# Queries and keys of twelve heads turned by DMA transposes of their 16-bit halves

## The chip, the cores and the metric

The kernel runs on one core of a Trainium2 chip. The core has five engines that work at the same time, each through its own queue in order: TensorE (PE; matrix products, results into PSUM), VectorE (DVE), ScalarE (ACT), GpSimd (POOL) and SyncE (SP, which here only issues DMAs). The metric is the device time in microseconds (us) of one execution; several runs are made and their median is given.

## The reference

One layer of a hybrid encoder over 256 tokens of width 2048, in float32:

```python
h = rms_norm(x)
p = h @ w_in                      # columns: qa, ka, va, fa (8 forget gates), qb, kb, vb
qa, ka = rms_norm per head        # 8 "fox" heads of width 128
out_a = softmax(qa.ka/sqrt(128) + c[t] - c[s], s <= t) @ va
out_b = stick_breaking(qb.kb/sqrt(128), s < t) @ vb          # 8 heads
x = x + concat(rms_norm(out_a), rms_norm(out_b)) @ w_out
x = x + ConvFFN(rms_norm(x))      # up 2048 -> 2 x 5632, causal conv, SiLU gate, down
```

The products q.k contract over the 128 features of a head, so q and k are needed with features on partitions and tokens along the free dimension. The projection leaves them the other way: a row tile holds 128 tokens on partitions and 4 heads x 128 features along the free dimension.

## The kernel before

**Products.** TensorE multiplies float32r data. To keep float32 accuracy each weight block of 128 x 2048 is loaded (w_raw, five buffers, issued by SyncE in `load`, L269), cast by ScalarE into a high part (w_hi, three buffers, `cast`, L275), and VectorE takes the rest (w_lo = w_raw - w_hi, `subtracted`, L283). `in_three` (L303) then makes three products per block: high with the activations' high and low parts (8 matmuls x 512 columns), and low with high (4 matmuls). So each block costs TensorE 12 matmuls, ScalarE one cast and VectorE one subtraction.

**Pieces.** The whole program is a list of steps (`steps`), each a weight block with its matmuls; here they are called pieces. The loop at the end emits, for piece n: evictions that are due (`following`), the cast and subtraction of piece n+2, the load of piece n+6, the matmuls of piece n, and then a tick. It thus writes out the order of each engine's queue by hand; nothing reorders it afterwards.

**Units.** After the fox values, five units of eleven pieces (0 to 10) project 512 + 512 columns each: unit 1 gives rows rA (q and k of fox heads 0 to 3), unit 2 rB (fox heads 4 to 7), unit 3 rC (q and k of stick-breaking heads 0 to 3), unit 4 the values vB, unit 5 rD (q and k of stick-breaking heads 4 to 7). A unit computes seven products for eight quarter blocks; the pieces 3, 5, 8 and 10 are double (24 matmuls, with a tick in the middle), the others single (12). Banks are called bank_a, bank_b, bank_c and bank_e. Pieces 0, 1, 2 and 3 of a unit open on bank_a, bank_c, bank_b and bank_e.

**Heads.** Beside the pieces run generators that are advanced once per tick. `fox_rows` and `sb_rows` take a finished unit's rows: the fox rows are normalised (squares on ScalarE, L662; a factor per head; the multiplication on VectorE, L672), and then `to_heads` transposes q and k: for k and then q, eight 128 x 128 transposes on TensorE into two PSUM tiles ps_h (L649), and a tick later two ScalarE evictions (L653), which also scale, into a tile kA, qA, kB or qB of 128 x 4 heads x 256 tokens (two buffers). After that one head every three ticks starts: scores ps_s (L744 to L750), exponentials (L762, L763), transposition ps_p (L774), eviction pT and p (L779, L780), product with the values ps_o (L721, L723), eviction oFox and its squares (L789, L727, L730). The stick-breaking heads have ps_z in place of ps_s. A gate sets when a half may be transposed: `started["fox"]` counts the fox heads whose scores have been emitted; rB waits for four, rC for eight.

In unit 5's first pieces the values are finished: `values_done` casts vB to its high part on ScalarE (L709) once VectorE has added the last bank (L605).

Of the kernel before, what the change touches and what calls it, by code (L numbers as in the profile page):

```python
# [8 lines left out]

F32 = mybir.dt.float32  # L10
F32R = mybir.dt.float32r
AF = mybir.ActivationFunctionType
ALU = mybir.AluOpType
AX = mybir.AxisListType

P = 128
D = 2048
S = 256
NT = S // P
KT = D // P  # L20
HD = 128
NH = 8
# [6 lines left out]
QSCALE = HD ** -0.5  # L29
# [17 lines left out]
def hybrid_layer(  # L47
# [19 lines left out]
    nc = tc.nc  # L67
    act, dve = nc.scalar, nc.vector
# [21 lines left out]
    class Early:  # L90
        n = 0
# [20 lines left out]
    gq = const.tile([P, 1], F32, name="gq")  # L112
    ccol = const.tile([P, 4, NC2], F32, name="ccol")
    R2 = const.tile([P, S], F32, name="R2")
    rstd1 = const.tile([P, NT], F32, name="rstd1")
    headR = const.tile([P, NH], F32R, name="headR")
    nrstd1 = const.tile([P, NT], F32, name="nrstd1")
    hT = big.tile([P, KT, 2, S], F32R, name="hT")
    xp = xf.rearrange("(t p) d -> p t d", p=P)
# [20 lines left out]
    g_q, g_k = pcol[:, 48:49], pcol[:, 49:50]  # L140
# [24 lines left out]
    def rsqrt(out_, ss, scale, n, gap=2):  # L165
        a = small.tile([P, n], F32, name="rs_a", tag=f"rs_a{n}")
        y = small.tile([P, n], F32, name="rs_y", tag=f"rs_y{n}")
        u = small.tile([P, n], F32, name="rs_u", tag=f"rs_u{n}")
        dve.tensor_scalar(a, ss, scale, EPS, op0=ALU.mult, op1=ALU.add)
        for _ in range(gap):  # L170
            yield
        act.activation(y, a, AF.Ln)
        act.activation(y, y, AF.Exp, scale=-0.5)
        dve.tensor_tensor(u, a, y, op=ALU.mult)
        dve.tensor_tensor(u, u, y, op=ALU.mult)
        dve.tensor_scalar(u, u, -0.5, 1.5, op0=ALU.mult, op1=ALU.add)
        dve.tensor_tensor(out_, y, u, op=ALU.mult)
# [20 lines left out]
    def split_tokens(ps, k, g, n=2):  # L198
        for j in range(n):
            i = k + j  # L200
            act.activation(hT[:, i, 0, :], ps[:, j, :], AF.Identity, scale=g[:, i : i + 1])
        for j in range(n):
# [6 lines left out]
    def squares(ss, c, junk):  # L209
        for t in range(NT):  # L210
            act.activation(
                junk, x2[:, t, c * 512 : (c + 1) * 512], AF.Square, accum_out=ss[:, t, c : c + 1]
            )
# [58 lines left out]
    def cast(raw, n, copy):  # L272
        hi = whi.tile([P, 2048], F32R, name="w_hi", tag="w_hi")
        lo = wlo.tile([P, 2048], F32R, name="w_lo", tag="w_lo")
        copy(hi[:, :n], raw[:, :n])  # L275
        return hi, lo
# [60 lines left out]
    oFox = late.tile([P, NH, S], F32, name="oFox")  # L337
    oSb = []
    ssq = [late.tile([P, S], F32, name=f"ssq{i}") for i in range(2)]
    masksR = at.tile([P, 4 * P], F32R, name="masksR")  # L340
    ntri = masksR[:, 2 * P :]
    maskF, maskB = (f32(masksR[:, i * P : (i + 1) * P]).unsqueeze(1).to_broadcast([P, 2, P]) for i in range(2))
    lf = at.tile([P, 4, NT, NH], F32, name="lf")[:, 0]
    chi = at.tile([P, S], F32R, name="chi")
    cR = at.tile([P, 3 * P], F32R, name="cR")
# [3 lines left out]
    def heads_tile(name):  # L349
        return at.tile([P, 4, S], F32, name=name, tag="qk", bufs=2)  # L350
# [8 lines left out]
    def evict_values(ps, c0, n):  # L359
        hi, lo, v1 = (v[:, c0 : c0 + n] for v in tile_of["vA"])  # L360
        act.activation(hi, ps[0][:, :n], AF.Identity, scale=rstd1[:, 0:1])
        act.activation(v1, ps[1][:, :n], AF.Identity, scale=rstd1[:, 1:2])

# [10 lines left out]
    started = {"fox": 0, "sb": 0}  # L374

    tile_of = {}
# [258 lines left out]
    def row_tiles(name, which):  # L635
# [2 lines left out]

        return make

    def to_heads(rows, keys, scales):

        for n in (1, 0):
            dst = tile_of[keys[n]] = heads_tile(keys[n])
            pss = []
            for t in range(NT):
                ps = psb.tile([P, 4, P], F32, name="ps_h", tag="t")
                for h in range(4):
                    nc.tensor.transpose(ps[:, h, :], rows[n, t][:, h * HD : (h + 1) * HD], ident)  # L649
                pss.append(ps)  # L650
            yield
            for t in range(NT):
                act.activation(dst[:, :, t * P : (t + 1) * P], pss[t], AF.Identity, scale=scales[n])  # L653

    def fox_rows(half):
        def done(rows):
            order = [(1, 0), (1, 1), (0, 1), (0, 0)]
            ss = small.tile([P, 4, 4], F32, name="ss", tag="ss")
            rn = small.tile([P, 4, 4], F32, name="rn", tag="rn")
            for m, nt in enumerate(order):  # L660
                for h in range(4):
                    act.activation(  # L662
                        zeros, rows[nt][:, h * HD : (h + 1) * HD], AF.Square,
                        accum_out=ss[:, m, h : h + 1],
                    )
                if m < 3:
                    yield
            flat = "p a b -> p (a b)"
            yield from rsqrt(rn.rearrange(flat), ss.rearrange(flat), 1.0 / HD, 16)
            for m, nt in enumerate(order):  # L670
                r3 = rows[nt].rearrange("p (h d) -> p h d", h=4)
                dve.tensor_tensor(r3, r3, rn[:, m, :].unsqueeze(2).to_broadcast([P, 4, HD]), op=ALU.mult)  # L672
                if m % 2:
                    yield
            while started["fox"] < 4 * half:
                yield
            yield from to_heads(rows, (f"qA{half}", f"kA{half}"), (gq, g_k))
            for h in range(4 * half, 4 * half + 4):
                waiting.append(fox_head(h, half))

        return done

    def sb_rows(half):
        def done(rows):
            while started["fox"] < NH or started["sb"] < 4 * half:
                yield
            if half:
                yield
                yield
            yield from to_heads(rows, (f"qB{half}", f"kB{half}"), (QSCALE, 1.0))  # L690
            ready.add(f"qB{half}")
            if "vB" in ready:
                start_sb(half)

        return done

    def start_sb(half):
        for h in range(4 * half, 4 * half + 4):
            waiting.append(sb_head(h, half))
# [737 lines left out]
```

## Time and profile before

| | |
|---|---|
| median of 3 runs (lowest, highest) | 1094.15 us (1093.35, 1094.19) |
| the profiled execution: its time, its span | 1093.69 us, 1091.6 us |
| busy: PE, PE weight loads, DVE, ACT, POOL | 1087.1, 939.8, 924.1, 755.3, 59.0 us |
| granted TensorE clock | 1.00 |
| moved by DMA | 258.53 MB, mean 237 GB/s |

"L275" is line 275 of the kernel before; a row such as `w_hi<-w_raw` names what is written and what is read, `x8` a number of instructions. Rows of the timeline begin with the start in us and the duration in us; adjacent equal instructions are merged, and `[1.33 <-PE ps_o L723]` says that the engine was idle for 1.33 us before and what ended that. The ends of matmuls are modelled, so the time from one start to the next is the better measure.

### The profile page before, as it was taken

The numbers are of one execution on the slowest core, as the hardware profiler recorded it, in microseconds if no ns is written. First come the engines' busy times: TensorE is split into PE (matmuls) and PEld (weight loads), VectorE is DVE, ScalarE is ACT, GpSimd is POOL, SyncE is SP. The second block draws the span as 40 slices with busy tenths as digits, with TensorE's granted clock in tenths as the row PEclk, the third lists the DMA queues.
The fourth block names the chain that finished last, engine by engine and source line by source line (L and its number), as shares of the span: only waits on it lengthen the run. The fifth ranks groups of instructions, "written<-read, shape, count | busy, mean of one in ns | idle before, by whom it ended". The sixth has DMA issues, their size and how long they took to land.

```text
span 1091.6 us, 14672 instructions
## 1 busy us (share of the span) xinstructions
PE 1087.1 (100%) x5701; PEld 939.8 (86%) x5701; DVE 924.1 (85%) x918; ACT 755.3 (69%) x968; POOL 59.0 (5%) x53
## 2 busy tenths in 40 slices
PE   9999999999999999999999999999999999999998
PEld 9988888888888888888888888888888888888887
DVE  5988899888897667779887988889898889879996
ACT  6767697767766657767766776677667667667763
POOL 0000000001000000000000000100000000000000
PEclk9999999999999999999999999999999999999999
DMA  8897886868777464669989597996979699895995
GB/s 310 275 271 240 271 205 205 246 192 265 236 215 250 154 199 160 212 173 248 289 204 316 176 264 253 255 296 170 301 197 282 229 246 281 212 319 163 295 251 149
DMA packets 175216, 258.53 MB, mean 237 GB/s; under 512 B 4633, under 2 KB 98219, under 8 KB 175147
## 3 DMA queue, kind: packets, MB, share of 16 engines
q1 hardware_dynamic: 151690, 210.26, 56.7%
q0 software_dynamic: 23280, 47.19, 24.5%
q8 instruction: 45, 0.74, 0.3%
q14 instruction: 25, 0.20, 0.0%
q10 hardware_dynamic: 176, 0.14, 0.0%
HBM read 255.48 MB, written 2.10 MB: 236 GB/s over the span
## 4 chain that ended last, share of the span: by engine, by line
PE 100%; DVE 0%; issue 0%
PE pu L1171 45%; PE bank_a L303 18%; PE bank_b L303 11%; PE bank_c L303 6%; PE acc_o L303 6%; PE acc_v L423 4%; PE bank_e L303 2%; PE acc L303 2%; PE ps_x L193 1%; PE ps_h L649 1%; PE ps_o L721 1%; PE ps_z L802 0%; PE ps_o L723 0%; PE ps_i L187 0%; PE half L303 0%; PE ps_z L821 0%
## 5 line engine op out<-in xcount | busy, mean ns | idle before, releaser
L283 DVE TENSOR_TENSOR w_lo<-w_raw,w_hi 128x2048 fp32r<-128x2048 f32 (+2 forms) x251 | 556.1, 2219 | 123.7 <-ACT w_hi L275 122.5
L275 ACT CAST w_hi<-w_raw 128x2048 fp32r<-128x2048 f32 (+2 forms) x251 | 464.6, 1854 | 222.2 <-PE pu L1171 91.7
L1171 PE MATMUL pu<-hT,w_hi 128*128 128x512 f32 x1408 | 333.6, 390 | 0.0
L1171 PEld LDWEIGHTS pu<-hT,w_hi 128*128 128x128 f32 x1408 | 263.1, 188 | 53.5
L1171 PEld LDWEIGHTS pu<-hT,w_lo 128*128 128x128 f32 x1408 | 180.0, 191 | 6.5
L1171 PE MATMUL pu<-hT,w_lo 128*128 128x256 f32 x1408 | 182.1, 283 | 0.0
L1224 POOL DMA_DIRECT2D w_raw<-in_w_down_dram x31 | 39.8, 1302 | 715.4 <-DVE w_lo L283 384.9
L1096 ACT ACTIVATE tap<-up,ccol 128x256 f32<-128x256 f32 x176 | 74.6, 495 | 0.0
L303 PE MATMUL bank_a<-w_hi,hT 128*128 128x512 f32 x192 | 48.6, 395 | 0.0
L303 PEld LDWEIGHTS bank_a<-w_hi,hT 128*128 128x128 f32 x192 | 35.2, 188 | 6.8
L303 PE MATMUL bank_a<-w_hi,s 128*128 128x512 f32 x160 | 40.0, 392 | 0.0
L303 PE MATMUL bank_b<-w_hi,s 128*128 128x512 f32 x160 | 40.0, 392 | 0.0
L303 PE MATMUL bank_a<-w_hi,g 128*128 128x512 f32 x152 | 38.0, 392 | 0.0
L423 PE MATMUL acc_v<-w_hi,hT 128*128 128x344 f32 x192 | 35.9, 329 | 0.0
L303 PEld LDWEIGHTS bank_b<-w_hi,s 128*128 128x128 f32 x160 | 28.9, 189 | 5.2
L303 PEld LDWEIGHTS bank_a<-w_hi,s 128*128 128x128 f32 x160 | 28.9, 189 | 5.2
L1101 DVE TENSOR_TENSOR val<-val,tap 128x512 f32<-128x512 f32 x44 | 30.3, 689 | 2.7 <-DVE val L1101 0.5
L1101 DVE TENSOR_TENSOR gate<-gate,tap 128x512 f32<-128x512 f32 x44 | 30.3, 689 | 2.6 <-DVE gate L1101 0.5
L303 PE MATMUL acc_o<-w_hi,oSb 128*128 128x512 f32 x128 | 31.8, 397 | 0.0
L1082 DVE TENSOR_TENSOR up<-t,R 128x512 f32<-128x512 f32 x44 | 30.5, 692 | 1.5
L303 PEld LDWEIGHTS bank_a<-w_hi,g 128*128 128x128 f32 x152 | 27.4, 189 | 4.9
L1089 ACT ACTIVATE gate<-up,ccol 128x256 f32<-128x256 f32 x44 | 24.1, 594 | 10.2 <-DVE s L1143 5.2
(293 smaller groups left out, 1413.9 us busy)
## 6 DMA issues: line engine op xcount, KB each, us to landing
w_raw<-in_w_up_dram SPq DMA_DIRECT2D x88, 1024.0 KB, 7.4
w_raw<-in_w_down_dram SPq DMA_DIRECT2D x44, 1024.0 KB, 6.6
w_raw<-in_w_in_dram SPq DMA_DIRECT2D x40, 1024.0 KB, 5.3
w_raw<-in_w_down_dram POOLq DMA_DIRECT2D x31, 1024.0 KB, 9.9
w_raw<-in_w_out_dram SPq DMA_DIRECT2D x16, 1024.0 KB, 7.6
w_raw<-in_w_in_dram POOLq DMA_DIRECT2D x10, 1024.0 KB, 9.8
w_raw<-in_w_in_dram SPq DMA_DIRECT2D x13, 516.0 KB, 5.0
xb<-in_x_dram POOLq DMA_DIRECT2D x4, 512.0 KB, 8.7
```

Of the source, the lines that this page charges most:

```text
L193: nc.tensor.transpose(ps[:, j, t * P : (t + 1) * P], x2[:, t, (k + j) * P : (k + j + 1) * P], ident)
L275: copy(hi[:, :n], raw[:, :n])
L283: dve.tensor_tensor(lo[:, :n], raw[:, :n], f32(hi[:, :n]), op=ALU.subtract)
L303: nc.tensor.matmul(o, lhs(i, l, t), r[:, i, :] if cut is None else r[:, i, cut], start=starts and j == 0, stop=stops and j == 3 * n - 1, s ...
L423: nc.tensor.matmul(banks[j][t][:, :VC], of_half(hT[:, k], l, t), w[:, 0, m * VC : (m + 1) * VC], start=k == l == 0 and w is mem["parts", i ...
L649: nc.tensor.transpose(ps[:, h, :], rows[n, t][:, h * HD : (h + 1) * HD], ident)
L1082: dve.tensor_tensor(u[:, :, 2:], t2, R, op=ALU.mult)
L1089: act.activation(a[:, j, :], u[:, j, 2:], AF.Identity, scale=ccol[:, 2, f : f + 1], bias=ccol[:, 3, f : f + 1],)
L1096: act.activation(taps[w][:, j, :], u[:, j, w : w + S], AF.Copy, scale=ccol[:, w, f : f + 1])
L1101: dve.tensor_tensor(a, a, tap, op=ALU.add)
L1171: nc.tensor.matmul(acc[:, j, S:] if low else acc[:, j, :], (lo if low else hi)[:, i, j * P : (j + 1) * P], hT[:, k, 0, :] if low else hT[: ...
L1224: nc.gpsimd.dma_start(mem[weights].rearrange("p (a b) -> p a b", a=4), plus, accum_op=ALU.add)
```

## The change

Three of the four transpositions (rA, rB and rC; twelve of the sixteen heads) no longer use TensorE. A float32 word is two 16-bit halves. `halves_out` lets ScalarE copy the rows so that all low halves stand in the first 512 columns and all high halves in the last 512 of a buffer of 1,024 16-bit columns, and issues, from ScalarE's queue, a DMA transpose of that buffer in blocks of 128 x 128, back onto the rows' own memory. It does so for two token tiles each of k and of q: four copies and four transposes of 256 KB per half. `halves_in` lets ScalarE copy the transposed halves into their places in kA, qA, kB or qB, again 1,024 16-bit elements per copy, and then scale the tile in place by one activation over 1,024 elements (not for kB, whose factor is 1).

For rA and rC the buffer of `halves_out` is the later kA, qA, kB or qB tile itself. For rB (`early`), which is sent before the gate opens, both k and q use the unused half of oFox, so q's copies wait until k's transposes have read it; a tick or two pass between k, q and the gate. For rC the gate is as before (eight fox heads), and k goes out in the tick in which it opens. rD keeps `to_heads`.

```diff
+    def halves_out(rows, n, buf):
+        for t in range(NT):
+            words = rows[n, t].bitcast(U16)
+            act.copy(
+                buf[:, t].rearrange("p (b f) -> p b f", b=2), words.rearrange("p (f b) -> p b f", b=2)
+            )
+            nc.scalar.dma_start_transpose(words.rearrange("p (g s) -> p g s", s=P), buf[:, t])
+
+    def halves_in(rows, n, dst, scale):
+        words = dst.bitcast(U16).rearrange("p h (s b) -> p b h s", b=2)
+        for t in range(NT):
+            act.copy(
+                words[:, :, :, t * P : (t + 1) * P],
+                rows[n, t].bitcast(U16).rearrange("p (b h s) -> p b h s", b=2, h=4),
+            )
+        if scale is not None:
+            act.activation(dst, dst, AF.Identity, scale=scale)
+
+    def sent_to_heads(rows, keys, scales, early, gate):
+        dst = {}
+
+        def own(n):
+            dst[n] = tile_of[keys[n]] = heads_tile(keys[n])
+            return dst[n]
+
+        if early:
+            room = oFox[:, 4:, :]
+            for n in (1, 0):
+                halves_out(rows, n, room.bitcast(U16).rearrange("p h s -> p (h s)").rearrange("p (t c) -> p t c", t=NT))
+                yield
+                yield
+            while gate():
+                yield
+        else:
+            while gate():
+                yield
+            for n in (1, 0):
+                halves_out(rows, n, own(n).bitcast(U16).rearrange("p h s -> p (h s)").rearrange("p (t c) -> p t c", t=NT))
+                yield
+            yield
+        for n in (1, 0):
+            if early:
+                own(n)
+            halves_in(rows, n, dst[n], scales[n])
+            yield
+
     def to_heads(rows, keys, scales):
...
-            while started["fox"] < 4 * half:
-                yield
-            yield from to_heads(rows, (f"qA{half}", f"kA{half}"), (gq, g_k))
+            yield from sent_to_heads(
+                rows, (f"qA{half}", f"kA{half}"), (gq, g_k), half == 1, lambda: started["fox"] < 4 * half
+            )
...
-            while started["fox"] < NH or started["sb"] < 4 * half:
-                yield
             if half:
+                while started["sb"] < 4:
+                    yield
                 yield
                 yield
-            yield from to_heads(rows, (f"qB{half}", f"kB{half}"), (QSCALE, 1.0))
+                yield from to_heads(rows, ("qB1", "kB1"), (QSCALE, 1.0))
+            else:
+                yield from sent_to_heads(
+                    rows, ("qB0", "kB0"), (QSCALE, None), False, lambda: started["fox"] < NH
+                )
```

Since the ticks shift, the change also moves head work. The places below show the queues; the lines of the changed kernel are about 50 further down than those before (L789 there is L738 before).

ScalarE's queue in unit 2, from the cast for its piece 7 on, before:

```order
L275 CAST w_hi<-w_raw 128x2048 x2
L653 ACTIVATE kA_1190<-ps_h,pcol 128x4x128 x2
L275 CAST w_hi<-w_raw 128x2048
L653 ACTIVATE qA_1222<-ps_h,gq 128x4x128 x2
L275 CAST w_hi<-w_raw 128x2048
L738 CAST qk<-qA_1222 128x128
L738 CAST qk<-kA_1190 128x256
L275 CAST w_hi<-w_raw 128x2048 x2
```

And now, behind the first of these two casts:

```order
L645 COPY kA_1190<-rA_754 128x1024
L648 DMA_TRANSPOSE rA_754<-kA_1190 128x8x128
L276 CAST w_hi<-w_raw 128x2048
L645 COPY qA_1214<-rA_752 128x1024
L648 DMA_TRANSPOSE rA_752<-qA_1214 128x8x128
...
L276 CAST w_hi<-w_raw 128x2048 x2
L653 COPY kA_1190<-rA_754 128x2x4x128
L658 ACTIVATE kA_1190<-kA_1190,pcol 128x1024
L653 COPY qA_1214<-rA_752 128x2x4x128
L658 ACTIVATE qA_1214<-qA_1214,gq 128x1024
L276 CAST w_hi<-w_raw 128x2048 x2
L789 CAST qk<-qA_1214 128x128
```

Each COPY and each DMA_TRANSPOSE stands there twice, for the two token tiles. The first head's qk casts now stand behind two more block casts, those for pieces 0 and 1 of unit 3.

TensorE's queue at the end of unit 4, before (piece 8 begins on bank_c):

```order
L303 MATMUL bank_c<-w_hi,hT 128x512 x8
L303 MATMUL bank_c<-w_lo,hT 128x512 x4
L774 MATMUL ps_p<-cs,pr 128x128 x3
L303 MATMUL bank_a<-w_hi,hT 128x512 x8
L303 MATMUL bank_a<-w_lo,hT 128x512 x4
```

And now:

```order
L304 MATMUL bank_c<-w_hi,hT 128x512 x8
L304 MATMUL bank_c<-w_lo,hT 128x512 x4
L772 MATMUL ps_o<-pT,vA_712 128x256 x2
L772 MATMUL ps_o<-pT,vA_713 128x256
L795 MATMUL ps_s<-cR,headR 128x384
L799 MATMUL ps_s<-qk 128x256 x3
L774 MATMUL ps_o<-p_2021,vA_714 128x128
L825 MATMUL ps_p<-cs,pr 128x128 x3
L801 MATMUL ps_s<-kA_1692,qA_1724 128x128
L304 MATMUL bank_a<-w_hi,hT 128x512 x8
L304 MATMUL bank_a<-w_lo,hT 128x512 x4
```

The scores of the last fox head, which stood in piece 5 of unit 4 before, now stand in its piece 8, and with them the opening of rC's gate.

ScalarE's queue behind that, now, up to the values' casts in unit 5:

```order
L276 CAST w_hi<-w_raw 128x2048
L653 COPY kB_2095<-rC_1368 128x2x4x128
L653 COPY kB_2095<-rC_1369 128x2x4x128
L840 ACTIVATE oFox<-ps_o,pcol 128x256
...
L653 COPY qB_2121<-rC_1366 128x2x4x128
L653 COPY qB_2121<-rC_1367 128x2x4x128
L658 ACTIVATE qB_2121<-qB_2121 128x1024
L619 ACTIVATE vB_1803<-bank_a,rstd_91 128x512
L276 CAST w_hi<-w_raw 128x2048
L830 CAST pT<-ps_p 128x256
L831 COPY p_2232<-ps_p 128x128
L760 CAST vB_2236<-vB_1804 128x512
L760 CAST vB_2236<-vB_1802 128x512
```

Before, the two evictions of kB and the two of qB stood in pieces 5 and 6 of unit 4; only head work, the eviction L618 and block casts stood in front of the values' casts.

More of the change, by code (lines that the diff above doesn't have):

```diff
@@ L11 @@
 F32R = mybir.dt.float32r
+U16 = mybir.dt.uint16
 AF = mybir.ActivationFunctionType
```

## The prediction

> **What bounds the kernel now.** I read the page's busy shares and its chain of waits first, then the busy time by stage.
>
> ```profile
> PE 1087.1 (100%) x5701; PEld 939.8 (86%) x5701; DVE 924.1 (85%) x918; ACT 755.3 (69%) x968; POOL 59.0 (5%) x53
> ...
> PE 100%; DVE 0%; issue 0%
> ```
>
> The chain that ends last is TensorE from end to end: what leaves TensorE's queue shortens the program, as long as nothing makes TensorE wait. The second view gives the stretches that the change touches (columns: TensorE, weight loads, VectorE, ScalarE, GpSimd, clock, DMA share, GB/s).
>
> ```profile
> core 0: us, PE busy (x) PEld busy (x) DVE busy (x) ACT busy (x) POOL busy (x), PEclk, DMA share, GB/s
> 137.00:160.00 23.00, 23.00 (x110) 19.32 (x109) 21.67 (x31) 21.77 (x62) 2.57 (x2) 1.00 0.80 180
> 113.00:237.00 124.00, 124.00 (x625) 105.16 (x624) 110.85 (x140) 91.51 (x164) 6.42 (x5) 1.00 0.76 225
> ```
>
> From 113 to 237 us ScalarE is idle for 124 - 91.5 = 32.5 us, but between 137 and 160 us for only 1.2 us. It casts each weight block, so work added to it can reach TensorE.
>
> **What is removed.** Six batches of eight transposes leave TensorE, two for each of the three halves (group A: rows rA, B: rB, C: rC).
>
> ```profile
> 112.74 1.98 PE L303 MATMUL bank_e<-w_hi,hT 128*128 128x512 f32 x8
> 114.55 1.07 PE L303 MATMUL bank_e<-w_lo,hT 128*128 128x512 f32 x4
> ...
> 118.18 1.03 PE L649 MATMUL ps_h<-cs,rA 128*128 128x128 f32 x8
> 118.97 2.08 PE L303 MATMUL bank_a<-w_hi,sums 128*128 128x512 f32 x8
> 120.88 1.07 PE L303 MATMUL bank_a<-w_lo,sums 128*128 128x512 f32 x4
> ```
>
> From start to start a batch takes 0.79 us. Eight wide products take 1.81 us (112.74 to 114.55), but 1.91 behind a batch. So a batch costs 0.89 and the six 5.3 us; a group costs 1.78. If nothing else waits, 1093.69 (the profiled execution's own time; the median of the three runs is 0.46 higher) becomes **1088.4**.
>
> **What is added to ScalarE.** Per group: four copies and four transposes issued ("out"), four copies and up to two scalings ("in"); four evictions of ps_h go.
>
> ```profile
> L936 ACT CAST hT<-oFox 128x1024 fp32r<-128x1024 f32 x2 | 2.1, 1051 | 0.6 <-PE bank_a L303 0.6
> 243.21 3.70 ACT L275 CAST w_hi<-w_raw 128x2048 fp32r<-128x2048 f32 x2
> 119.29 1.26 ACT L653 ACTIVATE kA<-ps_h,pcol 128x512 f32<-128x512 f32 x2
> 1088.61 0.38 ACTq L1195 DMA_DIRECT2D out_dram<-xb  x1
> L1224 POOL DMA_DIRECT2D w_raw<-in_w_down_dram x31 | 39.8, 1302 | 715.4 <-DVE w_lo L283 384.9
> ```
>
> 1,024 elements take 1.05 us. Two casts of 1.90 take 3.70 together, so neighbours overlap by 0.1: a block cast counts 1.80 and a copy 0.96, but 1.05 where a transpose waits for its end (and 1.05 for a scaling by a column). "In" is then 2 x 0.96 + 1.05 = 2.97. In A and B that is 4 x 1.08 + 2 x 2.97 = 10.3 us a group, in C, whose k is not scaled, 9.2, less about 2.3 a group for the evictions (the 1.26 for two, overlapping the next): some 23 us in all, and twelve issues.
>
> How long ScalarE's queue is held by one transpose, **H**, no row shows. The bounds are the plain DMA on the same queue, 0.38, and GpSimd's issue, 1.30, where software makes the pieces. A transpose resembles the first by its queue and the second by its many small rows (1,024 of 256 bytes), so I take the middle, 0.84. "Out" is then 2 x (1.05 + 0.03 + H) = 2.16 + 2H for the two tiles of k or of q.
>
> [...] No run so far shows a transpose.
>
> **Group A.** A block cast must end 0.5 us before its piece starts on TensorE: w_lo takes 2.29 more on VectorE (a row under group C) and starts 0.03 behind the cast, and it is wanted after the eight w_hi products, 1.81 later.
>
> ```profile
> 115.37 1.29 DVE L672 TENSOR_TENSOR rA<-rA,rn 128x512 f32<-128x512 f32 x2
> ...
> 133.57 0.34 PE L744 MATMUL ps_s<-cR,headR 128*128 128x384 f32 x1
> ...
> 134.24 2.09 PE L303 MATMUL bank_a<-w_hi,hT 128*128 128x512 f32 x8
> ...
> 139.79 1.98 PE L303 MATMUL bank_a<-w_hi,hT 128*128 128x512 f32 x8
> ```
>
> The first k rows are ready at 116.0. ScalarE's new order from there: out k, cast 1.80, out q, two casts 3.60, in k and in q 5.94, and the cast for piece 0 of unit 3, 1.91. It ends at 116.0 + 13.25 + 4.32 + 4H = 133.6 + 4H. Piece 0 started at 139.79; it now starts 1.78 earlier, and another 0.78 because the first head's scores (133.57 to 134.24, and the 0.11 behind them) come after it now: 137.2, so the cast must end by 136.7. Late by 0 (H 0.38), 0.2 (0.84), 2.1 (1.30).
>
> **Group B** sits behind the stretch in which ScalarE is full.
>
> ```profile
> 158.11 0.37 ACT L762 ACTIVATE pr<-ps_s,nm 128x128 f32<-128x128 f32 x1
> ...
> 158.91 0.22 ACT L172 ACTIVATE rs_y<-rs_a 128x16 f32<-128x16 f32 x1
> 161.94 1.29 DVE L672 TENSOR_TENSOR rB<-rB,rn 128x512 f32<-128x512 f32 x2
> 191.30 0.52 PE L721 MATMUL ps_o<-pT,vA 128*128 128x256 f32 x3
> ...
> 192.55 2.09 PE L303 MATMUL bank_c<-w_hi,hT 128*128 128x512 f32 x8
> 211.40 0.47 ACT L789 ACTIVATE oFox<-ps_o,pcol 128x256 f32<-128x256 f32 x1 [1.33 <-PE ps_o L723]
> ...
> 212.44 1.12 ACT L653 ACTIVATE kB<-ps_h 128x512 f32<-128x512 f32 x2
> ```
>
> A pair of exponentials takes 0.80 (158.11 to 158.91), the end of one head with the next copies 1.04 (211.40 to 212.44). Out starts at about 162.4 (rows ready, as before). To the cast for piece 1 of unit 4 the order holds two outs, four more casts, two pairs of exponentials, one head's end and two ins: 17.7 + 4.32 + 4H, so 184.4 + 4H. That piece started at 192.55, is 3.56 earlier by groups A and B, and has 1.92 of head work less in front (191.30 to 192.55 is 1.25, and another head's scores 0.67): 187.1, cast due 186.6. Late by 0, 1.2, 3.0, of which group A has already given 0, 0.2, 2.1; piece 2, whose cast follows 3.85 us of work later and is due 3.6 later, adds 0.3. A and B together: **0, 1.5, 3.3**.
>
> **Group C** decides most.
>
> ```profile
> 237.17 1.91 ACT L275 CAST w_hi<-w_raw 128x2048 fp32r<-128x2048 f32 x1 [1.12 <-PE bank_c L303]
> 242.10 0.63 ACT L709 CAST vB<-vB 128x512 fp32r<-128x512 f32 x1 [2.50 <-DVE vB L605]
> 242.63 0.68 ACT L599 ACTIVATE rD<-bank_a,rstd 128x512 f32<-128x512 f32 x1
> ...
> 241.32 0.75 DVE L605 SCALAR_TENSOR_TENSOR vB<-bank_c,rstd,vB 128x512 f32<-128x512 f32 x1
> 245.14 2.29 DVE L283 TENSOR_TENSOR w_lo<-w_raw,w_hi 128x2048 fp32r<-128x2048 f32 x1 [0.87 <-ACT w_hi L275]
> ...
> 243.31 1.98 PE L303 MATMUL bank_b<-w_hi,sums 128*128 128x512 f32 x8
> 246.61 2.08 PE L303 MATMUL bank_e<-w_hi,hT 128*128 128x512 f32 x8
> 248.53 1.07 PE L303 MATMUL bank_e<-w_lo,hT 128*128 128x512 f32 x4
> ```
>
> In unit 5 the cast for piece 2 (237.17) starts a fixed train: w_lo, the vB eviction behind it on VectorE, the vB cast that waits for it, an eviction, the cast for piece 3 (243.21), w_lo (245.14 to 247.43). The w_lo products of piece 3 start at 248.53, 1.1 later; so piece 3 can start at 246.61 - 1.1 = 245.5 at the earliest, 8.33 after the start of piece 2's cast. Out k now waits for the last head's scores to have read the buffer that kB takes. Back from piece 2 (243.31 - 5.3 = 238.0) over six products of 2.72, their three 0.11 and head work of 2.16, these end at 219.2. Then: out k, a head's end 1.04, out q, cast 1.80, exponentials 0.80, cast 1.80, in k 1.92, a head's end 1.04, in q 2.9, the vB eviction 0.58 (242.63 to 243.21), and piece 2's cast starts at 219.2 + 11.9 + 4.32 + 4H = 235.4 + 4H. Piece 3 starts 8.33 later: 245.3, 247.1, 248.9 against 246.61, or **-1.3, +0.5, +2.3**. So even at the shortest H the train gives back 4 of the 5.3 us.
>
> The sum: 0 - 1.3, 1.5 + 0.5, 3.3 + 2.3, so 1092.4, **1095.6** and 1099.3. About 0.2% (2.2 us) is what a measurement of this kernel can tell from no change.
>
> **Rivals.** *TensorE keeps its saving* (faster). For it: 32.5 idle ScalarE microseconds against 23 and the issues; TensorE waits nowhere in these stretches now. Against it: the train in unit 5. It needs the walk to be a microsecond too long, and H below 0.4: 1088.4 to 1091.9, say 1090.
>
> *The issue holds ScalarE* (slower). Twelve transposes stand in an in-order queue, and from 0.84 to 1.30 the sum rises by 3.7, 8 us per us of H. It decides from H of about 0.95, where the sum passes 1096.3; at 1.30 it gives 1099.3. For it speaks GpSimd's 1.30, against it the 0.38. [...]
>
> *The transposes land late* (slower).
>
> ```profile
> out_dram<-xb SPq DMA_DIRECT2D x7, 256.0 KB, 2.3
> w_raw<-in_w_in_dram POOLq DMA_DIRECT2D x10, 1024.0 KB, 9.8
> ...
> q1 hardware_dynamic: 151690, 210.26, 56.7%
> ```
>
> The walks leave 6.3 us (group B, where the second q copy overwrites what k's second transpose reads) to 9.2 between an issue and its waiter. A 256 KB store lands in 2.3, so I count nothing; at 9.8, as behind GpSimd's loads, some 3 us are missing in each group: 1095.6 + 9 = 1105. The last row gives 65 ns of an engine per packet of 1.4 KB (0.567 x 16 x 1091.6 / 151690). By bytes the twelve transposes are 12% more than the 27 MB that the stretch moves anyway (225 GB/s x 124 us), and fit into the quarter of the DMA time that is free (share 0.76); were each of their 12,288 rows to cost a packet's 65 ns, they would take 50 us of the 16 engines against 30 free, and weights could come 20 late.
>
> **Chances.** No change (my forecast) 0.40. Faster 0.24. Slower 0.36: the held queue 0.2, late landing 0.08, a walk that is too short (VectorE is 94% busy between 137 and 160) 0.08. The range runs from most of the saving, 1089.5, to H past 1.30 or a little late landing, 1102.
>
> **What would show it.** Right: ps_h rows of TensorE only for rD, about 5.3 us less; DMA_TRANSPOSE rows on ScalarE's queue of 0.4 to 1.3 us; TensorE idle behind w_hi or w_lo in pieces 1 to 3 of units 4 and 5; piece 3 of unit 5 starting within 3 us of 246.6, and all later pieces shifted by as much. Wrong: that piece at 241.5 (the saving stands), copies far from 1.05 us, or ScalarE waiting for the transposes' DMAs.

## The result and the profile after

The change makes the kernel slower: **1122.05 us** (median of 4 runs, 1119.18 to 1124.83) against 1094.04 (1093.35 to 1094.19), a ratio of 1.0257 with a 95% interval of 1.0227 to 1.0287. Predicted were 1095.6, in a range up to 1102. The profiled execution has a span of 1121.6 us against 1091.6, so 30.0 us are to be found in it.

The page's busy times and its chain of waits, of the kernel after:

```profile
PE 1093.0 (97%) x5653; PEld 940.8 (84%) x5653; DVE 924.3 (82%) x918; ACT 778.9 (69%) x985; POOL 59.0 (5%) x53
...
PE 82%; ACT 3%; issue 1%; ACTq 1%; DMA 1%; DVE 0%; DVEq 0%
```

TensorE's busy time did not fall by the 5.3 us saved. It rose by 5.9, although 48 matmuls are gone, so some matmuls run slower; and 28.6 us of the span are idle, where there were 4.5. TensorE no longer makes up the whole chain.

The stretches of the kernel after where this happens (the columns as in the prediction; the seventh number is the granted clock):

```profile
120.00:140.00 20.00, 11.67 (x42) 8.54 (x41) 8.78 (x7) 13.41 (x10) 0.00 (x0) 0.83 1.04 237
200.00:220.00 20.00, 17.31 (x80) 14.52 (x81) 19.40 (x26) 16.29 (x29) 2.31 (x2) 0.91 0.76 177
240.00:260.00 20.00, 12.79 (x56) 10.46 (x55) 9.18 (x11) 14.38 (x21) 1.28 (x1) 0.87 0.47 108
260.00:280.00 20.00, 16.40 (x62) 13.38 (x62) 11.95 (x11) 13.06 (x17) 0.58 (x1) 0.78 0.56 151
```

Before, TensorE was busy for all of 113 to 237 us at clock 1.00 (the row in the prediction). The two largest losses lie at groups A and C. The loss by the lowered clock is busy time x (1 - clock): 2.0 + 1.6 + 1.7 + 3.6 = 8.9 us in these four rows, an estimate, since the clock of a row is a mean over its idle time too.

TensorE's timeline after, its longest gaps and the products behind them:

```profile
135.39 3.71 PE L304 MATMUL bank_a<-w_hi,hT 128*128 128x512 f32 x8 [7.50 <-DVE rB L606]
138.94 1.08 PE L304 MATMUL bank_a<-w_lo,hT 128*128 128x512 f32 x4
...
256.93 0.87 PE L825 MATMUL ps_p<-cs,pr 128*128 128x128 f32 x3 [7.21 <-DVE pr L817]
...
269.26 0.80 PE L772 MATMUL ps_o<-pT,vA 128*128 128x256 f32 x2 [3.60 <-DVE pT L832]
...
276.22 2.09 PE L304 MATMUL bank_e<-w_hi,hT 128*128 128x512 f32 x8
```

None of the three waits is for the weights of TensorE's next piece, where the prediction looked. TensorE waits for VectorE: for an addition (L606) that frees bank_a, for a head's normalised exponentials (pr) and for a head's pT. After 7.50 us of idleness eight products take 3.55 us (135.39 to 138.94), not 1.81. The last row is piece 3 of unit 5, predicted within 3 us of 246.6.

ScalarE's own timeline shows where VectorE's work was held up (`[1.61 <-issue]` is time in which the engine waited for nothing but its queue; ACTq is that queue):

```profile
116.03 1.05 ACT L645 COPY kA<-rA 128x1024 uint16<-128x1024 uint16 x1 [0.66 <-DVE rA L719]
117.11 1.54 ACTq L648 DMA_TRANSPOSE rA<-kA  x1
118.69 1.05 ACT L645 COPY kA<-rA 128x1024 uint16<-128x1024 uint16 x1 [1.61 <-issue]
119.77 2.53 ACTq L648 DMA_TRANSPOSE rA<-kA  x1
122.40 1.91 ACT L276 CAST w_hi<-w_raw 128x2048 fp32r<-128x2048 f32 x1 [2.66 <-issue]
124.21 1.04 ACT L645 COPY qA<-rA 128x1024 uint16<-128x1024 uint16 x1
125.28 2.71 ACTq L648 DMA_TRANSPOSE rA<-qA  x1
128.03 1.04 ACT L645 COPY qA<-rA 128x1024 uint16<-128x1024 uint16 x1 [2.79 <-issue]
129.11 1.25 ACTq L648 DMA_TRANSPOSE rA<-qA  x1
130.45 3.70 ACT L276 CAST w_hi<-w_raw 128x2048 fp32r<-128x2048 f32 x2 [1.38 <-issue]
```

VectorE at the same place, after, and (the last two rows) at group C:

```profile
126.55 0.75 DVE L606 SCALAR_TENSOR_TENSOR rB<-bank_e,rstd,rB 128x512 f32<-128x512 f32 x1
132.38 2.29 DVE L284 TENSOR_TENSOR w_lo<-w_raw,w_hi 128x2048 fp32r<-128x2048 f32 x1 [5.09 <-ACT w_hi L276]
134.59 0.74 DVE L606 SCALAR_TENSOR_TENSOR rB<-bank_a,nrstd,rB 128x512 f32<-128x512 f32 x1
...
251.77 2.29 DVE L284 TENSOR_TENSOR w_lo<-w_raw,w_hi 128x2048 fp32r<-128x2048 f32 x1 [6.11 <-ACT w_hi L276]
...
256.50 0.29 DVE L817 TENSOR_SCALAR pr<-pr,rl 128x128 f32<-128x128 f32 x1
```

The addition that frees bank_a has nothing to do with the block that is being cast. But it stands behind that block's w_lo in VectorE's in-order queue, and w_lo waits for the cast of 130.45, which stands behind four copies and four transposes. Thus ScalarE's queue holds up VectorE's, and VectorE's holds up TensorE. At group C it is the same: w_lo waits 6.11 us for a cast that stands behind four copies and four transposes, a sum of blocks follows, and only then comes the pr for which TensorE waits 7.21 us.

### The profile page after: what moved, and what is told of

Its sections match the earlier page's. It is cut to its first block, busy times and chain, and to the rows that moved or that the text cites. A ratio compares the mean times of both kernels' runs of the same rounds, so it can differ in the third digit from the quotient of the medians.

```text
span 1121.6 us, 14605 instructions
## 1 busy us (share of the span) xinstructions
PE 1093.0 (97%) x5653; PEld 940.8 (84%) x5653; DVE 924.3 (82%) x918; ACT 778.9 (69%) x985; POOL 59.0 (5%) x53
## 3 DMA queue, kind: packets, MB, share of 16 engines
q10 hardware_dynamic: 12848, 3.29, 1.7%
## 4 chain that ended last, share of the span: by engine, by line
PE 82%; ACT 3%; issue 1%; ACTq 1%; DMA 1%; DVE 0%; DVEq 0%
PE pu L1222 44%; PE bank_a L304 14%; PE bank_b L304 8%; PE acc_o L304 6%; PE bank_c L304 4%; PE acc L304 2%; PE bank_e L304 1%; ACT w_hi L276 1%; ACTq L648 1%; PE ps_o L772 0%; DMA rB<-oFox 0%; PE ps_x L194 0%; PE ps_z L853 0%; ACT oFox L645 0%; PE ps_o L774 0%
## 5 line engine op out<-in xcount | busy, mean ns | idle before, releaser
L304 PE MATMUL bank_a<-w_hi,hT 128*128 128x512 f32 x192 | 52.1, 416 | 9.0 <-DVE rB L606 7.5
L304 PE MATMUL bank_c<-w_hi,hT 128*128 128x512 f32 x120 | 31.9, 410 | 0.6 <-ACT w_hi L276 0.6
```

What stands on the lines that cost most here:

```text
L304: nc.tensor.matmul(o, lhs(i, l, t), r[:, i, :] if cut is None else r[:, i, cut], start=starts and j == 0, stop=stops and j == 3 * n - 1, s ...
```

## The experiments

The theories: **hold** (each transpose keeps ScalarE's in-order queue for 1.25 to 2.7 us), **copies** (the added work on ScalarE suffices) and **landing** (somebody waits for transposed data). Later: **late heads** (the heads start two to four ticks later).

**Copies without transposes.**

```diff
-            nc.scalar.dma_start_transpose(words.rearrange("p (g s) -> p g s", s=P), buf[:, t])
```

> The changed kernel without its twelve DMA transposes; all of ScalarE's copies and scalings stay, and the copies back read each row's interleaved halves as they are. So q and k of twelve heads are left untransposed. Hold (each transpose keeps ScalarE's in-order queue for 1.64 us in the mean, 19.7 us in all, and casts, VectorE's products of the low halves and its additions come late one after the other): without it the gaps of 7.5 us (waiting for rB, 128 us) and 7.2 us (waiting for pr, 257 us) go, and the time is 1089 to 1096. Copies (the 26 us of copies and scalings by themselves make the casts late): 1112 or more, and both gaps stay. Landing (somebody waits for the transposed data): 1089 to 1096 too; the next kernel parts it from the hold.

Measured: 1101.45 us (1100.95 to 1102.13), ratio 1.0069 [1.0052, 1.0086], so 7.6 us over before and 20.6 under the change. This lies between the expectations: the transposes cost most, but the copies are not free. The gap for rB fell from 7.5 to 0.5; one in group C stayed. TensorE, ScalarE and VectorE there, without transposes:

```profile
248.41 0.80 PE L771 MATMUL ps_o<-pT,vA 128*128 128x256 f32 x2 [4.87 <-DVE pT L831]
...
236.74 2.63 ACT L652 COPY qB<-rC 128x1024 uint16<-128x1024 uint16 x2
239.41 1.06 ACT L657 ACTIVATE qB<-qB 128x1024 f32<-128x1024 f32 x1
240.37 0.67 ACT L619 ACTIVATE vB<-bank_a,rstd 128x512 f32<-128x512 f32 x1
240.94 1.89 ACT L276 CAST w_hi<-w_raw 128x2048 fp32r<-128x2048 f32 x1
...
242.87 2.29 DVE L284 TENSOR_TENSOR w_lo<-w_raw,w_hi 128x2048 fp32r<-128x2048 f32 x1 [3.88 <-ACT w_hi L276]
245.08 0.74 DVE L606 SCALAR_TENSOR_TENSOR vB<-bank_c,rstd,vB 128x512 f32<-128x512 f32 x1
245.74 2.28 DVE L592 TENSOR_TENSOR w_raw<-w_raw 128x2048 f32<-128x2048 f32 x1
247.94 0.42 DVE L831 TENSOR_TENSOR pT<-ps_p,pT 128x256 fp32r<-128x256 f32 x1
```

The same pattern: a late cast (240.94), and behind it on VectorE w_lo, an addition, a sum of blocks and then the small pT for which TensorE waits.

**Transposes without copies.** The kernel before with twelve transposes of a constant tile added on ScalarE's queue, into rows that nobody reads again.

```diff
+            if keys[n] not in ("qB1", "kB1"):
+                for t in range(NT):
+                    nc.scalar.dma_start_transpose(
+                        rows[n, t].bitcast(U16).rearrange("p (g s) -> p g s", s=P), masksR.bitcast(U16)
+                    )
```

> The kernel before, with TensorE's transposes and ScalarE's evictions as they were, and twelve DMA transposes of a constant tile issued behind the evictions of the same three halves, into row tiles that nobody reads again. Nothing waits for what they write and no copy is added. Hold: TensorE gets gaps behind VectorE's additions again and granted clocks below 0.8 after them; two issues stand together four and four, after the evictions and not between, so I expect less than the 28 us of the change, 1101 to 1116. Copies: 1094 to 1097. Landing: 1094 to 1097.

Measured: 1104.43 us (1103.64 to 1105.78), ratio 1.0095 [1.0080, 1.0110], as expected for the hold. Transposes that nobody waits for cost 10.6 us. TensorE's waits, and the durations of the transposes in ns (min/median/max):

```profile
PE ps_s L754 <- DVE qk L745: 2.6, 1, 2.6
PE bank_a L304 <- DVE vB L606: 2.2, 1, 2.2
PE bank_a L304 <- DVE rB L606: 1.9, 1, 1.9
...
L657 ACTq DMA_TRANSPOSE rA<-masksR x4: 1511/3166/6180, 119.8 to 127.9; - x4
L657 ACTq DMA_TRANSPOSE rB<-masksR x4: 1248/2264/3575, 174.1 to 180.1; - x4
L657 ACTq DMA_TRANSPOSE rC<-masksR x4: 1340/1668/5150, 220.9 to 229.7; - x4
```

Here transposes follow each other without a copy between, and one of them holds the queue for up to 6.2 us.

**Transposes on another queue.**

```diff
-            nc.scalar.dma_start_transpose(words.rearrange("p (g s) -> p g s", s=P), buf[:, t])
+            nc.sync.dma_start_transpose(words.rearrange("p (g s) -> p g s", s=P), buf[:, t])
```

> The changed kernel with the transposes issued on SyncE's queue instead of ScalarE's; every copy stays. SyncE's queue carries the weight loads, which wait in it for free buffers, so a transpose can be issued late there and weight loads behind it late too. Hold: the copies on ScalarE follow each other without the 1.25 to 2.7 us between them, and the time is 1091 to 1102, by how long the transposes stand behind weight loads. Copies: 1112 or more. Landing: 1120 or more, since the data come later still than now.

Measured: 1102.45 us (1102.07 to 1102.61), ratio 1.0075 [1.0060, 1.0090]: 0.45 above the upper end for the hold and far from the other two. It is within 1.0 us of the form without any transposes: the data movement itself costs about 1 us, and its place in ScalarE's queue some 20 us. Landing plays a small part: ScalarE waits once, for 1.2 us, for rA<-qA.

**One group at a time,** with the transposes on ScalarE's queue and the other groups as before:

> The change for group A (rA) alone; rB's and rC's q and k are transposed on TensorE as before. Hold: the gap of 7.5 us in unit 2 stands as it is (it comes from group A's own transposes and copies), with about 4 us of lowered clock behind it and 1.8 us saved on TensorE: 1094.0 + 7.5 + 0.6 + 4 - 1.8 = 1104, between 1101 and 1107. If my walk of the prediction were right that group A alone costs next to nothing and only the later groups add up: 1092 to 1095.

> The change for group B (rB, sent early) alone. In the profile of the whole change TensorE's gaps between 180 and 206 us are 1.5 (rC's addition), 0.3, 1.1 and 1.7 us (the heads' pT), with a granted clock of 0.91 in that stretch, about 6.5 us in all, and 1.8 us are saved. If the groups cost independently of each other: 1094 + 6.5 - 1.8 = 1098.7. If B's gaps came from what group A left late, or B's buffer wait is covered by its early start: 1092 to 1095.

> The change for group C (rC) alone. If the groups are independent, what A (9.0 us) and B leave of the 28 us: 1094 + 14 = 1108, between 1105 and 1111, with gaps of some 7 us waiting for pr and 4 us waiting for pT. If C's gaps are mostly inherited from A and B: 1096 to 1102. If C's train costs what my prediction's walk said (piece 3 of unit 5 at most 2.3 us late): 1094 to 1096.5.

Measured: A 1102.86 us (+9.0, ratio 1.0080 [1.0065, 1.0095]), B 1099.21 (+5.6, 1.0057 [1.0040, 1.0074]), C 1102.38 (+8.8, 1.0079 [1.0064, 1.0094]). The sum, 23.4, is 4.6 less than the 28.0 of all three, so most of the cost is each group's own; C alone costs 8.8 and not the 14 expected. In A alone the gap for rB is 7.04. C alone starts its transposes 26 us earlier than in the whole change (213.0 for 239.0 us) and meets other waits there; TensorE's timeline shows a plain late cast:

```profile
226.86 3.78 PE L304 MATMUL bank_c<-w_hi,hT 128*128 128x512 f32 x8 [5.07 <-ACT w_hi L276]
233.36 2.11 PE L304 MATMUL bank_a<-w_hi,hT 128*128 128x512 f32 x8 [1.27 <-DVE vB L606]
```

**Spreading the copies back** (SyncE's queue, group C).

```diff
         for t in range(NT):
+            if t and spread:
+                yield
             act.copy(
```

> The kernel with the transposes on SyncE's queue (1102.45 us), in which group C's four copies back are now emitted one per tick instead of two, so that casts of weight blocks stand between them; nothing is added or removed. Place (what hurts is that q's copies and scaling, 3.7 us, stand in one stretch ahead of the cast of piece 2 of unit 5, from which VectorE's product, addition, sum of blocks and pT follow in order): the gap of 4.9 us waiting for pT goes to under 1.5 and the granted clock stays near 1: 1094 to 1098. Amount (ScalarE simply has too much work there, wherever it stands): 1100 to 1104.

Measured: 1106.53 us, ratio 1.0120 [1.0105, 1.0135], 4.1 *slower* than unspread. Both expectations missed. The gap for pT halved (4.87 to 2.32), but new ones came, 1.84 (rD's eviction) and 4.4 in two (ws, a tile of the stick-breaking heads, at 280 and 303 us). Why ws is late was not tested.

**The hold by itself.** In the feed-forward part of the kernel before, sizes 128, 256, 512 and 896 columns in turn.

```diff
+            nc.scalar.dma_start_transpose(
+                turned[1][:, :c].rearrange("p (g s) -> p g s", s=P), turned[0][:, :c]
+            )
```

> The kernel before, with twelve DMA transposes of a constant tile in the feed-forward part on ScalarE's queue, of 128, 256, 512 and 896 columns of 16 bits, three each, one at a time, five pieces apart. It measures the time for which one holds the queue, and its landing, when nothing else is issued there. [...] Where the 1.25 to 2.7 of the change come from a transpose that follows another closely, all of these are at their lowest.

Measured (ScalarE's timeline, the second round of the four sizes in their order):

```profile
526.71 1.14 ACTq L1376 DMA_TRANSPOSE turned<-turned  x1
549.81 1.19 ACTq L1376 DMA_TRANSPOSE turned<-turned  x1
570.02 1.21 ACTq L1376 DMA_TRANSPOSE turned<-turned  x1
590.80 1.24 ACTq L1376 DMA_TRANSPOSE turned<-turned  x1
```

One that stands alone holds the queue for 1.14 to 1.24 us, at 128 columns as at 896, and the third round reads the same (in the first, 512 and 896 columns took 1.85 and 1.42). The hold is a cost per issue, not per column; what comes on top is met where several are issued within a few us. The kernel takes 1093.8 us in its one run, against 1093.59: at these places twelve holds cost nothing that can be seen.

**The same holds, placed otherwise** (group A alone, ScalarE's queue): q's first tile a tick earlier.

```diff
-            for n in (1, 0):
-                halves_out(rows, n, ...)
-                yield
-            yield
+            for tiles in (((1, 0),), ((1, 1), (0, 0)), ((0, 1),)):
+                for n, t in tiles:
+                    ...
+                    halves_out(rows, n, ..., (t,))
+                yield
```

> Group A alone, transposes on ScalarE's queue as in the change, but q's first copy and transpose now stand a tick earlier, with k's second, so that over three ticks one, two and one of them stand between casts in place of two, two and none; the same instructions otherwise, and k's and q's copies back in the same tick as before. The cast from which the gap of 7.0 us follows (129.5 us in group A alone) then has three copies and transposes ahead of it and not four: one copy of 1.05 and one hold of 1.25 to 2.3 fewer. Hold, by way of VectorE's queue and bank_a: the gap shrinks by about 3 us to 4, the clock falls less behind it, and the time falls from 1102.9 to 1097 to 1100. If TensorE waits for something else than that cast (the amount of held time, 7.2 us in the group, or the landing): 1102 to 1104.

Measured: 1102.30 us (1101.81 to 1103.81), ratio 1.0080 [1.0066, 1.0094], no better than A alone and within the second range, not the first. The first part of the mechanism answered: the cast came 2.1 earlier (127.44 us; one transpose now held for 3.42), and so did VectorE's addition and TensorE's products (132.38 for 134.48), though the gap shrank only from 7.04 to 5.83. But the casts behind the copies back did not come earlier (140.75 for 140.40), and a gap of 2.10 for qk at 150 us, which A alone does not have, takes the gain back. Removing one wait uncovers the next.

**Fewer scalings.** SyncE's queue, the factor of the fox k multiplied into that of q, groups B and then A and B:

```diff
-        dve.tensor_scalar(gq, g_q, QSCALE, None, op0=ALU.mult)
+        dve.scalar_tensor_tensor(gq, g_q, QSCALE, g_k, op0=ALU.mult, op1=ALU.mult)
```

> The change for group B alone, its transposes on SyncE's queue, and the fox heads' two scalings made one: the factor of k is multiplied into that of q, so that kA needs no scaling after its copies back. 1.8 us leave TensorE; with the transposes on SyncE's queue TensorE's gaps at this group were 0.4 and 0.9, and 1.15 us less of ScalarE's work should shorten them. Hold: 1091.5 to 1094, the first form that could beat the kernel before. If ScalarE's copies alone cost what they save: 1093.5 to 1095.

> The same with groups A and B. 3.6 us leave TensorE; with SyncE's queue the gaps of A and B were 0.45 (rB's addition), 2.4 (qk), 0.3, 0.4 and 0.9, together 4.4. Without the scaling of k each group has 1.15 us less on ScalarE: 1091 to 1095.

Measured: B 1093.82 us, ratio 0.9999 [0.9990, 1.0008]; A and B 1096.30, 1.0022 [1.0013, 1.0031]. B is as fast as before, in the overlap of its two ranges; A and B miss theirs. In B the saving can be watched coming and going on TensorE:

```profile
163.02 2.08 PE L304 MATMUL bank_b<-w_hi,hT 128*128 128x512 f32 x8
...
172.12 2.09 PE L304 MATMUL bank_c<-w_hi,hT 128*128 128x512 f32 x8
...
256.28 2.08 PE L304 MATMUL bank_e<-w_hi,hT 128*128 128x512 f32 x8
```

Before, these started at 162.29, 173.19 and 255.45: 0.73 late, then 1.07 early (1.80 saved, as the prediction's 1.78), then 0.83 late. It is lost between 190 and 252 us with no gap over 0.4, in a stretch where the second half's heads run 10.2 us later than before.

**Copies out on GpSimd** (SyncE's queue, all groups).

```diff
-            act.copy(
+            nc.gpsimd.tensor_copy(
                 buf[:, t].rearrange("p (b f) -> p b f", b=2), words.rearrange("p (f b) -> p b f", b=2)
```

> All three groups, transposes on SyncE's queue, and the twelve copies ahead of the transposes on GpSimd instead of ScalarE, which takes 12.6 us off ScalarE. No row so far shows such a copy on GpSimd. Amount of ScalarE's work: the gap of 4.9 us in group C shrinks and the time falls from 1102.5 to 1095 to 1100. If GpSimd needs several us for a copy, the data come late or q's copies back do: 1102 to 1112.

Measured: 1100.82 us, ratio 1.0065 [1.0052, 1.0079], between the two expectations. A copy takes 1.1 to 2.3 us there. C's gap fell to 3.7, but A and B got gaps of 2.06 and 1.97 for rB and rC. Twelve copies fewer on ScalarE gave 1.6 us.

**Late heads.** The kernel before with empty ticks ahead of its own transposes, in all groups and in B alone:

```diff
+            for _ in range(2 if half else 3):
+                yield
             yield from to_heads(rows, (f"qA{half}", f"kA{half}"), (gq, g_k))
```

> The kernel before, with nothing sent by DMA and no copy added: its transposes on TensorE only stand 3, 2 and 3 ticks later (groups A, B, C), as far as the change moves the start of the heads behind its copies out and back. Late heads (the copies' loss of 7.6 us comes less from their time on ScalarE than from heads that start later and so fall into unit 5, whose casts, additions and sums then wait for one another): 1099 to 1107, with a gap near unit 5's first pieces. Copies: 1094 to 1096.

> The kernel before with group B's transposes alone 4 ticks later, the delay that the change has there (first scores of the second half 10.2 us later). With group B sent on SyncE's queue with one scaling 1.8 us were saved and given back between 243 and 252 us without a gap over 0.4. Late heads: the delay alone costs what was given back, 1095 to 1096.5. If the copies cost it: 1093.5 to 1094.5.

Measured: 1095.24 us for all (1.0013 [1.0004, 1.0023]) and 1095.63 for B by four ticks (1.0019 [1.0010, 1.0028]). In B the delay costs 2.1 us, about what was given back there (1.07 + 0.83). In all groups it costs 1.7, although the first scores of the two fox halves then start about as late (141.61 and 193.75 us) as in the form with the copies and without transposes (140.81 and 194.45; before, 133.57 and 181.82). So late heads do not explain the 7.6 of the copies; their time on ScalarE is left for that, which is an argument by elimination and no test.

**Tighter.** Sent into their own tiles, copies back one tick after the copies out:

> Group B alone on SyncE's queue with one scaling (1093.82 us), but sent into its own tiles, and with the copies back one and two ticks behind the copies out, so that the heads start two ticks later than before and not four. Late heads: part of what was given back stays, 1092 to 1093.4. Copies: 1093.5 to 1094.5. Landing: if the copies back now wait for the transposes, 1095 or more.

> The same with groups A and B (1096.30 us before tightening). Late heads: 1091.5 to 1095. Copies: 1096 to 1098. Landing: 1098 or more, with ScalarE waiting for DMAs of rA and rB.

Measured: B 1093.39 us (1092.85 to 1093.81), ratio 0.9999 [0.9991, 1.0008]; A and B 1102.91, 1.0087 [1.0073, 1.0100]. B cannot be told from before, nor from the looser form. With A, ScalarE waits for landings (its group lines):

```profile
L653 ACT COPY qA<-rA 128x1024 uint16<-128x1024 uint16 x2 | 2.6, 1347 | 1.6 <-DMA rA<-qA 1.6
L653 ACT COPY kA<-rA 128x1024 uint16<-128x1024 uint16 x2 | 2.6, 1344 | 1.0 <-DMA rA<-kA 1.0
```

With 0.8 for rB's q these waits sum to 3.4 us; the looser form of A and B waited 2.2. TensorE's gaps grew to 4.0 for pT and 3.2 for qk. The range expected for landing is met, but that landing alone costs the 6.6 us between the two forms was not tested.

No form that was tried beats the kernel before.

## Why the prediction was wrong

**What held.** TensorE's queue bounds the kernel (100% of the chain before, 82% after), and a batch of transposes is worth 0.89 us (two of them measured 1.80). "Out" copies cost 1.05. Nobody waits for a transpose in the changed kernel: the "in" copies show no idle time before them, though the landing is 4.6 to 8.0 us and not the 2.3 counted. The rows are a small load on the DMA engines: the row of the profile's page for ScalarE's queue after

```profile
q10 hardware_dynamic: 12848, 3.29, 1.7%
```

gives 24 ns per packet (0.017 x 16 x 1121.6 / 12848), not the 65 that I feared. The likeliest slow rival, *the issue holds ScalarE*, names the main cause and its point (H above 0.95); it had a chance of 0.2 and a price of 1099.3.

**The first wrong step: H.** The bounds were 0.38 and 1.30, and I took 0.84. By lines of the kernel after (ns):

```profile
L648 ACTq DMA_TRANSPOSE rB<-oFox x4: 1248/1306/1442, 172.1 to 183.8; - x4
L648 ACTq DMA_TRANSPOSE rA<-kA x2: 1537/2034/2532, 117.1 to 119.8; - x2
L648 ACTq DMA_TRANSPOSE rA<-qA x2: 1248/1981/2714, 125.3 to 129.1; - x2
L648 ACTq DMA_TRANSPOSE rC<-kB x2: 1784/1934/2084, 239.0 to 242.2; - x2
L648 ACTq DMA_TRANSPOSE rC<-qB x2: 1247/1252/1257, 246.2 to 248.6; - x2
```

Mean 1.64, sum 19.7 us: outside the bounds. The plain DMA on the same queue (0.38) was no measure of it, and GpSimd's 1.30 (its loads are the page's queue q0, software_dynamic) is near the shortest hold, not the longest. By the prediction's own slope of 8 us per us of H, 1.64 gives 1102.0. So the size of H is worth 6.4 of the 26.5 us by which the forecast missed, and the forecast would still have been some 20 us short.

**The second wrong step, and the larger one: the due rule.** "A block cast must end 0.5 us before its piece starts on TensorE" looks only at the piece's own weights. VectorE executes in order: the addition for bank_a began at 134.59 us, behind the w_lo that had begun at 132.38 after 5.09 us of waiting for its cast. Behind a late w_lo stand the additions that free banks, and the heads' qk, pr and pT; TensorE wants those before it wants that w_lo. For group A I counted at most 2.1 us late; TensorE waited 7.5 at the bank_a half of piece 8, before the piece that I was looking at. For group C I counted -1.3 to +2.3, by a train from one cast to piece 3; 7.2 and 3.6 us went at pr and pT. The form without transposes is the same test at H = 0: only group C's walk still moves below H = 0.38, so the walks give 1092.4 - 4 x 0.38 = 1090.9; measured were 1101.45.

**A term that was too small: the "in" copies.** Two of them with a scaling were counted as 2.97; in groups A and B they took 3.61 to 3.69 up to the start of what follows. Two copies alone take 2.53 to 2.60, and a scaling up to 1.15. Over the three groups that is 3.9 us more on ScalarE. Put into my walks together with each group's own four holds (8.0, 5.3 and 6.4 us), it makes A 6.2 us late, B no later than A already is, and piece 3 of unit 5 another 4.6 us late: 1093.7 + 10.8 = 1104.5, an estimate. So both sizes explain about a third of the miss, and the larger part remains for the due rule and the clock.

**A term that was missing: the clock.** After TensorE's gaps of 7.5, 7.2 and 3.6 us the next eight wide products took 3.55 or 3.56 us each time, and the windows lose 8.9 us to granted clocks of 0.78 to 0.91. Behind each the clock was about half of full speed: 3.55 for 1.81 us, and granted clocks of 0.51 between 135 and 139 us, 0.50 between 257 and 260.5, and 0.50 between 269 and 273. A gap of 2.08 us in group B alone was followed by a lower clock too (last section). So a gap costs more than its length: behind each of these three, eight products alone took about 1.7 us longer.

**The account.** TensorE's listed gaps after are 0.64, 0.19, 7.50, 1.53, 0.31, 1.10, 1.72, 7.21 and 3.60, together 23.8; with the estimated 8.9 for the clock and less 5.3 saved that makes 27.4 of the 30.0 us between the two profiles. By experiments, against the change without its saving (28.0 + 5.3 = 33.3): copies alone 7.6 + 5.3 = 12.9, holds added to them 20.4. Holds alone, though longer (33 us in sum), cost 10.6; so the two are dear together, because the copies use up the room in which a hold would do no harm. That last clause is read from these three numbers, and was not tested by itself.

## What to carry to other kernels

Before adding work to an in-order engine with idle time, follow its late output through the *next* engine's queue: all that stands behind the waiting instruction is late too, and the bound engine may need one of those first. A DMA transpose issued from ScalarE's queue cost ScalarE 1.25 to 2.7 us here, so price an issue by a measured one of the same kind, and let several following each other count more than one alone (up to 6.2 us each here, for 1.14 to 1.24). ScalarE's idle share of 26% over the whole stretch did not help here: what counted was how late single casts came.

## What the runs showed of the hardware

A 16-bit DMA transpose within SBUF holds the issuing queue for about 1.2 us when it stands alone (ten of twelve; the others 1.42 and 1.85), whatever its size from 128 to 896 columns. With a 1.05 us copy between, holds were 1.25 to 2.7 in the changed kernel and up to 3.42 in group A alone with q's first tile a tick earlier; without one, up to 6.2. On SyncE's queue the same holds appear (1.24 to 4.19 with all groups). What lengthens a hold stays open: it may be the DMAs still in flight, or the load on the DMA engines (share 1.04 between 120 and 140 us after, 0.70 before).

Whether the transposes slow the weight loads is not shown. The profile's median landing for the 40 loads of w_in on SyncE's queue is 5.3 us before and 7.2 after, but it knows the landing of only some of them, and not of the same ones. Loads known in both differ little: the one issued at about 57 us took 9.8 before and 9.9 after, the one of 176.6 us before and 189.6 after took 5.1 and 5.4. One that was issued amid group A's transposes took 7.5 us, for 5.3 before.

TensorE's clock also fell after gaps much shorter than 7.5 us: 2.08 us (group B alone) were followed by eight products in 3.38 us instead of 1.81, and the granted clock between 160 and 180 us was 0.92, while behind 1.97 (copies on GpSimd) and 2.42 (spread copies) eight took 1.95 and 1.93. TensorE's rows for group B alone:

```profile
176.54 3.58 PE L304 MATMUL bank_a<-w_hi,hT 128*128 128x512 f32 x8 [2.08 <-DVE rC L606]
179.92 1.24 PE L304 MATMUL bank_a<-w_lo,hT 128*128 128x512 f32 x4
```

A ScalarE copy of 1,024 16-bit elements that writes to every second place takes 1.32 to 1.38 us in the changed kernel, and two in a row 2.53 to 2.60; one that reads so and writes densely takes 1.05, and two in a row 2.00 (transposes on SyncE's queue).
